# Twelve low parts at the four feed-forward entries: from VectorE subtractions to accumulating transfers

## The chip, the cores and the metric

The kernel runs on one core of one Trainium2 chip. The core has TensorE (PE, with its weight loads shown apart as PEld), VectorE (DVE), ScalarE (ACT), GpSimd (POOL) and SyncE (SP), and 16 DMA engines. The time is the device time of one execution in microseconds (us), median of several runs. All durations below come from one execution taken by the hardware profiler.

## The reference

The reference computes two blocks on x of 512 tokens by 1024 channels in float32. Each block has two mixers, and each mixer is followed by a feed-forward part, so there are four of these:

```
def swiglu(h, wg, wu, wd):
    return (jax.nn.silu(h @ wg) * (h @ wu)) @ wd
```

follows the hybrid mixer and the conformer convolution (hidden size 2816), and

```
def sq_relu_mlp(x, w_up, w_down):
    return jnp.square(jax.nn.relu(x @ w_up)) @ w_down
```

follows the differential attention and the short convolution (hidden size 4096). All operands are float32, and the result must hold float32 accuracy, which is why each weight and each activation is split into a high and a low part.

## The kernel before, in words

The activations lie transposed: channels on partitions, the 512 tokens along the free side, in eight tiles of 128 channels. Each float32 matmul is made of three matmuls in the fp32r format (`mm3`, L302 to L305): high weight by high activation (L303), high weight by low activation (L304), low weight by high activation (L305). The `wl` in a row's L305 is thus the low part of a weight, and it is the last of the three that is needed.

`w_parts` (L269 to L281) makes both parts of a weight chunk of 128x1024 floats (512 KB) that lies in SBUF as loaded (`wraw`). ACT copies it into `wh`, which rounds it (all ACT rows carry line 102, since a helper issues them). Then the low part is made in one of two ways: DVE subtracts, `wl = wraw - wh` (L279); or, where the flag `low_by_dma` is set, ACT writes the chunk scaled by -1, rounded, into `wl`, and a transfer on the POOL queue adds the chunk to it in memory (L277, `accum_op=add`). Before, the flag is set in one place only, the first projection of the conformer convolution, for 16 chunks. `wh` and `wl` have four buffers each, `wraw` three (each of two chunks, 1 MB).

A feed-forward's first matrix is worked off in groups of 512 output columns. The first group is `group_plain` (L488): eight k steps of 128 rows of the weight, two halves of the tokens (`th` 0 and 1, 256 tokens each), 12 matmuls of 128x256 per k step and half, so 96 per half. Its weights are two row blocks of 1 MB, k 0 to 3 and k 4 to 7, which are four chunks #1 to #4 of two k steps each. At given k steps it calls other work (norms: L423 in the swiglu, L1127 in the MLP, both on PE at th 0 behind k 3). All further groups are `group_s` (L513): a scheme with seven block products in place of eight, each product 24 matmuls of 128x256 with one weight chunk of 128x4x256. Its blocks b11, b12, b21, b22 are halves of two loaded `wraw` buffers, and sums of them are formed in place on DVE: b11 becomes b12-b11 (L530), b12 becomes b22-b12 (L539), b22 becomes b11-b22 with the new b11 (L540). The first product is called o11 here and uses b11 as loaded; the second uses the new b11 (b11' here), the third the new b22 (b22' here), the fourth b22 as loaded (o22 here).

I call the start of a feed-forward, `group_plain` and the first `group_s` behind it, an entry. In the profile PE begins the plain group of the four entries at about 304 us (swiglu 1), 873 us (swiglu 2), 1488 us (MLP 1) and 2040 us (MLP 2). Around an entry DVE also makes the low parts of the activations (L430, L435, L456), the sums of activations that `group_s` multiplies (L454 to L464), the squares' sum of the norm (L412), and takes the results from PSUM (L849, L852 in the swiglu). In the MLP, DVE applies the norm before it (L1135, L1136, with the factor `rm` that ACT makes from PE's L1127). A scheduler (the Tile framework) orders the instructions of each engine from the program's dependences; an engine works its own list in order, so an instruction that waits holds all behind it.

Of the kernel before, what the change touches and what calls it, by code (L numbers as in the profile page):

```python
# [109 lines left out]
def body(ctx: ExitStack, tc: tile.TileContext, A, out, consts):  # L110
# [11 lines left out]
    def bank(tag="mm"):  # L122
        n_ps[0] += 1
        return pp.tile([P, T], F32, tag=tag, name=f"ps{n_ps[0]}", bufs={"mm": 4, "at": 4}[tag])
# [11 lines left out]
    def F(n=1):  # L136
        r = [fslots.pop(0) for _ in range(n)]
        return r if n > 1 else r[0]
# [126 lines left out]
    n_p = [0]  # L265

    low_by_dma = [False]

    def w_parts(src, n):  # L269
        n_p[0] += 1  # L270
        wh = wpool.tile([P, 1024], F32R, tag="wh", name=f"wh{n_p[0]}", bufs=4)
        wl = wpool.tile([P, 1024], F32R, tag="wl", name=f"wl{n_p[0]}", bufs=4)
        v = (lambda t: t[:, :n]) if len(src.shape) == 2 else (lambda t: t[:, :n].rearrange("p (k c) -> p k c", k=src.shape[1]))
        act.activation(v(wh), src, AF.Copy)
        if low_by_dma[0]:
            act.activation(v(wl), src, AF.Copy, scale=-1.0)
            pool_e.dma_start(out=v(wl), in_=src, accum_op=ALU.add)  # L277
        else:
            dve.tensor_sub(v(wl), src, v(b(wh)))  # L279
        return wh, wl  # L280
# [21 lines left out]
    def mm3(ps, wh, wl, h, l, start, stop):  # L302
        pe.matmul(ps, wh, h, start=start, stop=False, skip_group_check=True)  # L303
        pe.matmul(ps, wh, l, start=False, stop=False, skip_group_check=True)  # L304
        pe.matmul(ps, wl, h, start=False, stop=stop, skip_group_check=True)  # L305
# [168 lines left out]
    def load_blocks(w0, w1):  # L474

        rvs = []
        for kh in range(2):
            n_w[0] += 1
            raw = wpool.tile([P, 2048], F32, tag="wraw", name=f"wraw{n_w[0]}", bufs=3)
            rv = raw[:, :].rearrange("p (k c) -> p k c", k=4)  # L480
            rows = slice(kh * 512, (kh + 1) * 512)
            if w0[0] is w1[0] and w1[1] == w0[1] + 256:
                sync.dma_start(rv, w0[0][rows, w0[1] : w0[1] + 512].rearrange("(k p) c -> p k c", p=P))
            else:
                for n, (ap, c) in enumerate((w0, w1)):
                    sync.dma_start(rv[:, :, n * 256 : (n + 1) * 256], ap[rows, c : c + 256].rearrange("(k p) c -> p k c", p=P))
            rvs.append(rv)
        return rvs  # L488

    def group_plain(w0, w1, evac, at):  # L490


        ws = []
        for rv in load_blocks(w0, w1):
            for h in range(2):
                wh, wl = w_parts(rv[:, 2 * h : 2 * h + 2, :].rearrange("p k c -> p (k c)"), 1024)
                ws += [(wh[:, k * T : (k + 1) * T], wl[:, k * T : (k + 1) * T]) for k in range(2)]
        for th, tr in enumerate((T0, T1)):
            pss = [bank(), bank()]
            for k in range(8):  # L500
                for n in range(2):
                    for p in range(2):
                        wh, wl = (t[:, n * 256 + p * P : n * 256 + (p + 1) * P] for t in ws[k])
                        mm3(pss[n][:, p * 256 : (p + 1) * 256], wh, wl, xh[k][:, tr], xl[k][:, tr], k == 0 and p == 0, k == 7)
                if (th, k) in at:
                    at[th, k]()
            for n in (1, 0):
                evac(n, th, pss[n], False)

    def group_s(w0, w1, evac):  # L510


        bb = []  # L513
        for rv in load_blocks(w0, w1):
            bb += [rv[:, :, :256], rv[:, :, 256:]]
        b11, b12, b21, b22 = bb

        def product(ps, w, x, start=False):
            for k in range(4):
                for p in range(2):  # L520
                    wh, wl = (t[:, k * 256 + p * P : k * 256 + (p + 1) * P] for t in w)
                    mm3(ps[:, p * 256 : (p + 1) * 256], wh, wl, *x(k), start and k == 0 and p == 0, k == 3)

        xs = lambda k0, tr: lambda k: (xh[k0 + k][:, tr], xl[k0 + k][:, tr])
        sums = lambda n: lambda k: (so[0][:, k, n, :], so[1][:, k, n, :])
        parts = lambda t: w_parts(t, 1024)

        a, d, g = bank(), bank("at"), bank("at")
        o11 = parts(b11)
        dve.tensor_sub(b11, b12, b11)  # L530
        product(a, o11, xs(0, T0), True)
        p1 = F()
        act.activation(p1, a, AF.Copy)

        product(g, parts(b11), sums(0), True)
        p5 = F()
        act.activation(p5, g, AF.Copy)
        o22 = parts(b22)
        dve.tensor_sub(b12, b22, b12)  # L539
        dve.tensor_sub(b22, b11, b22)  # L540
        product(a, parts(b22), sums(1))
        u2 = F()
        act.activation(u2, a, AF.Copy)
        product(g, o22, sums(2))
        dve.tensor_add(u2, g, u2)
        evac(1, 0, u2, True)
        product(a, parts(b12), xs(0, T1))
        dve.tensor_add(p5, a, p5)
        evac(1, 1, p5, True)
        product(d, parts(b21), xs(4, T0), True)  # L550
        dve.tensor_add(p1, d, p1)
        evac(0, 0, p1, True)
        dve.tensor_add(b21, b21, b22)
        product(a, parts(b21), xs(4, T1))
        evac(0, 1, a, False)
# [267 lines left out]
    def swiglu(layer, nxt):  # L823
# [15 lines left out]
        for pi, nf in enumerate(parts):  # L839
            (ph, hh), (pl, hl) = RP(nf // 2), RP(nf // 2)  # L840
            for fc in range(nf // 2):
                col = (f0 + fc * 2) * P
                ss = [None, None]

                def evac(n, th, ps, own):
                    x = HALVES[th]
                    if n == 1:
                        s = ss[th] = ps if own else F()
                        dve.tensor_mul(halves_2(s), halves_2(ps), rb[:, x].unsqueeze(1).to_broadcast([P, 2, 256]))  # L849
                        act.activation(s, s, AF.Silu)  # L850
                        return
                    dve.tensor_mul(ss[th], ps, ss[th])  # L852
                    split_to(ph[fc][:, :, x], pl[fc][:, :, x], halves_2(ss[th]))
                    freeF(ss[th])
                    if own:
                        freeF(ps)

                if pi == 0 and fc == 0:
                    group_plain((wu, col), (wg, col), evac, {(0, 3): norm, (1, 0): lambda: split_all_sums("ffnn", layer)})
                    after_first()  # L860
                else:
                    group_s((wu, col), (wg, col), evac)
# [28 lines left out]
    w1 = A["cv_w_pw1"][0]  # L891
# [496 lines left out]
    def mlp(layer, nxt, before):  # L1388
# [4 lines left out]
        for pi in range(4):  # L1393
            (ph, hh), (pl, hl) = RP(4), RP(4)
            for g in range(2):
                f0 = pi * 8 + g * 4

                def evac(n, th, ps, own):
                    s = ps if own else F()
                    act.activation(s, ps, AF.Relu)  # L1400
                    act.activation(s, s, AF.Square)
                    split_to(ph[g * 2 + n][:, :, HALVES[th]], pl[g * 2 + n][:, :, HALVES[th]], halves_2(s))
                    freeF(s)

                if pi == 0 and g == 0:
                    group_plain((wu, f0 * P), (wu, f0 * P + 256), evac, {
                        (0, 1): before.second, (1, 0): lambda: split_all_sums("fpre", layer)})
                    for k in range(4):
                        split_s3(k, V("fpre", layer * 8 + k))
                    post = Post().then("fpost", layer, nxt) if nxt else Final("fpost", layer)  # L1410
                else:
                    group_s((wu, f0 * P), (wu, f0 * P + 256), evac)
# [105 lines left out]
```

## Time and profile before

| | |
|---|---|
| median of 3 runs | 2416.68 us (2415.71 to 2418.15) |
| profiled execution | 2416.4 us, span 2414.6 us, 1.8 us around it |
| mean granted TensorE clock | 0.991 |
| PE busy | 2362.9 us, 98% |
| DVE busy | 1562.3 us, 65% |
| ACT busy | 1195.4 us, 50% |
| POOL busy | 228.0 us, 9% |

The busy share tells that PE hardly ever idles. It idles 51.7 us in all (span less busy time), most of it in 36 waits, and the table of waits says which instruction of which engine ended them. A row of a timeline has the start, the duration, the engine, the line, the operation, the tiles (output first) and, in brackets, how long the engine was idle before and what ended that.

### The profile page before, as it was taken

How to read it: one execution, taken by the hardware profiler on the slowest of the kernel's cores; microseconds unless marked ns; L12 is line 12 of the kernel's file. 1: busy time of each engine (PE TensorE's matmuls, PEld its weight loads, DVE VectorE, ACT ScalarE, POOL GpSimd, SP SyncE). 2: the span in 40 equal slices, each digit the busy share in tenths (PEclk: the TensorE clock that was granted, in tenths of full speed). 3: DMA queues.
4: the chain of work that ended last, by engine and by line, in shares of the span. 5: the costliest groups of instructions: out<-in, count | busy, mean ns of one | idle time of the engine just before them, and what ended most of it. 6: DMA issues, size and time to landing. Idle time of an engine off the chain costs nothing. (4 is left out here: it accounts for less than half of the span.)

```text
span 2414.6 us, 34306 instructions
## 1 busy us (share of the span) xinstructions
PE 2362.9 (98%) x14087; PEld 2051.1 (85%) x14087; DVE 1562.3 (65%) x2099; ACT 1195.4 (50%) x2005; POOL 228.0 (9%) x206
## 2 busy tenths in 40 slices
PE   8999999999999899999999999899998999999998
PEld 6667798999887799898987778798898888888997
DVE  4334685867699978685746775664577544854664
ACT  4663463434675654352534555653554224653553
POOL 0000000111113110202000003100003102100001
PEclk9999999999999999999999999999999999999999
DMA  5112223242563023232331112222332222222330
GB/s 167 36 53 68 73 72 121 73 135 73 135 153 97 19 87 123 70 127 84 116 105 58 48 53 71 88 88 88 122 105 70 96 96 88 73 76 96 123 105 36
DMA packets 150415, 215.30 MB, mean 89 GB/s; under 512 B 6079, under 2 KB 88562, under 8 KB 150258
## 3 DMA queue, kind: packets, MB, share of 16 engines
q1 hardware_dynamic: 147921, 204.72, 26.3%
q0 software_dynamic: 2304, 8.39, 1.8%
q8 instruction: 110, 1.80, 0.3%
q14 instruction: 48, 0.39, 0.0%
q10 hardware_dynamic: 32, 0.01, 0.0%
HBM read 202.61 MB, written 2.10 MB: 85 GB/s over the span
## 5 line engine op out<-in xcount | busy, mean ns | idle before, releaser
L303 PE MATMUL ps<-rs,wh 128*128 128x256 f32 (+1 forms) x3216 | 1083.8, 337 | 10.4 <-ACT rs L102 5.1
L305 PE MATMUL ps<-rs,wl 128*128 128x256 f32 (+1 forms) x3216 | 1080.2, 336 | 10.3 <-DVE wl L279 10.3
L304 PE MATMUL ps<-rs,wh 128*128 128x256 f32 (+1 forms) x3216 | 1081.2, 336 | 0.0
L279 DVE TENSOR_TENSOR wl<-wraw,wh 128x1024 fp32r<-128x1024 f32 (+1 forms) x472 | 576.6, 1230 | 473.9 <-ACT wh L102 472.3
L102 ACT ACTIVATE wh<-wraw 128x1024 fp32r<-128x1024 f32 (+1 forms) x488 | 508.3, 1047 | 665.6 <-PE ps L304 528.1
L303 PEld LDWEIGHTS ps<-rs,wh 128*128 128x128 f32 x3216 | 609.9, 190 | 78.1 <-ACT rs L102 5.9
L305 PEld LDWEIGHTS ps<-rs,wl 128*128 128x128 f32 x3216 | 610.6, 190 | 77.1 <-DVE wl L279 11.8
L304 PEld LDWEIGHTS ps<-rs,wh 128*128 128x128 f32 x3216 | 610.4, 190 | 67.2 <-issue 2.9
L102 ACT ACTIVATE fs<-fs 128x512 f32<-128x512 f32 (+2 forms) x365 | 205.3, 571 | 87.8 <-DVE fs L1168 20.2
L305 PE MATMUL ps<-ph_so,wl 128*128 128x256 f32 x816 | 234.7, 288 | 3.1 <-DVE wl L279 2.9
L303 PE MATMUL ps<-ph_so,wh 128*128 128x256 f32 x816 | 233.3, 286 | 4.0 <-ACT wh L102 3.5
L304 PE MATMUL ps<-ph_so,wh 128*128 128x256 f32 x816 | 232.5, 285 | 0.0
L102 ACT ACTIVATE fs<-ps 128x512 f32<-128x512 f32 (+1 forms) x202 | 112.5, 561 | 136.3 <-PE ps L305 105.6
L305 PEld LDWEIGHTS ps<-ph_so,wl 128*128 128x128 f32 x816 | 158.2, 194 | 6.6 <-DVE wl L279 6.6
L303 PEld LDWEIGHTS ps<-ph_so,wh 128*128 128x128 f32 x816 | 158.4, 194 | 5.1 <-ACT wh L102 4.2
L304 PEld LDWEIGHTS ps<-ph_so,wh 128*128 128x128 f32 x816 | 158.1, 194 | 0.0
L102 ACT ACTIVATE rs<-fs 128x512 fp32r<-128x512 f32 (+1 forms) x153 | 91.9, 606 | 77.1 <-DVE fs L852 45.3
L435 DVE TENSOR_TENSOR rs<-fs,rs 128x512 fp32r<-128x512 f32 (+1 forms) x132 | 86.5, 662 | 17.2 <-ACT rs L102 16.8
L868 POOL TENSOR_TENSOR fs<-fs,fs 128x512 f32<-128x512 f32 x32 | 52.2, 1631 | 474.2 <-DVE fs L866 474.2
L102 ACT ACTIVATE rs<-fs,vec 128x256 fp32r<-128x256 f32 (+1 forms) x104 | 58.5, 585 | 62.6 <-POOL fs L1136 19.1
L412 POOL TENSOR_TENSOR fs<-fs,fs 128x512 f32<-128x512 f32 x28 | 46.5, 1662 | 382.3 <-ACT fs L102 376.2
L1106 POOL TENSOR_TENSOR fs<-fs,fs 128x256 f32<-128x256 f32 (+1 forms) x33 | 35.4, 1072 | 363.0 <-ACT fs L102 356.6
(310 smaller groups left out, 2209.7 us busy)
## 6 DMA issues: line engine op xcount, KB each, us to landing
wraw<-in_mlp_w_up_dram SPq DMA_DIRECT2D x32, 1024.0 KB
wraw<-in_mlp_w_down_dram SPq DMA_DIRECT2D x32, 1024.0 KB
wraw<-in_ffn_w_up_dram SPq DMA_DIRECT2D x44, 512.0 KB
wraw<-in_ffn_w_gate_dram SPq DMA_DIRECT2D x44, 512.0 KB
wraw<-in_ffn_w_down_dram SPq DMA_DIRECT2D x20, 1024.0 KB
wraw<-in_cv_w_pw_dram SPq DMA_DIRECT2D x16, 512.0 KB
wl<-wraw POOLq DMA_DIRECT2D x16, 512.0 KB, 5.3
wraw<-in_attn_w_qkv_dram SPq DMA_DIRECT2D x16, 512.0 KB
```

The costliest lines, as they stand in the source:

```text
L102: r = self.engine.activation(out, in_, func, **kw)
L279: dve.tensor_sub(v(wl), src, v(b(wh)))
L303: pe.matmul(ps, wh, h, start=start, stop=False, skip_group_check=True)
L304: pe.matmul(ps, wh, l, start=False, stop=False, skip_group_check=True)
L305: pe.matmul(ps, wl, h, start=False, stop=stop, skip_group_check=True)
L412: r = eng.tensor_add(acc, acc, s)
L435: dve.tensor_sub(l, src, b(h))
L868: pool_e.tensor_add(res[o], res[o], s)
L1106: pool_e.tensor_add(self.acc[:, tr], self.acc[:, tr], s[:, tr])
```

## The change

A second flag, `after_plain`, is added. In `group_plain`, the chunks of the second row block (#3 and #4, k 4 to 7) get their low parts by the accumulating transfer, and so does o11 of the first `group_s` behind it. That is three chunks at each of four entries: 12 subtractions on DVE (L279) go, 12 ACT copies and 12 POOL transfers (L277) come. No load and no matmul is added or removed.

```diff
+    after_plain = [False]
...
-        for rv in load_blocks(w0, w1):
+        for i, rv in enumerate(load_blocks(w0, w1)):
+
+            low_by_dma[0] = i == 1
             for h in range(2):
                 wh, wl = w_parts(rv[:, 2 * h : 2 * h + 2, :].rearrange("p k c -> p (k c)"), 1024)
...
+        low_by_dma[0] = False
+        after_plain[0] = True
...
         a, d, g = bank(), bank("at"), bank("at")
+        low_by_dma[0], after_plain[0] = after_plain[0], False
         o11 = parts(b11)
+        low_by_dma[0] = False
         dve.tensor_sub(b11, b12, b11)
```

The flags add lines, so a line of the kernel before stands 1 higher in the changed one from L267 on and 7 higher from L530 on (L279 becomes L280, L530 becomes L537).

DVE at entry 1, before, from the low part of o11 (`wl_2354`, from `wraw_2344`) to L540:

```order
L279 TENSOR_TENSOR wl_2354<-wraw_2344,wh_2353 128x1024
L456 SCALAR_TENSOR_TENSOR rs_69<-fs_99,vec,rs_65 128x256
L456 SCALAR_TENSOR_TENSOR rs_70<-fs_108,vec,rs_66 128x256
L530 TENSOR_TENSOR wraw_2344<-wraw_2344 128x4x256
L456 SCALAR_TENSOR_TENSOR rs_70<-fs_109,vec,rs_66 128x256
L539 TENSOR_TENSOR wraw_2344<-wraw_2347,wraw_2344 128x4x256
L279 TENSOR_TENSOR wl_2384<-wraw_2344,wh_2383 128x1024
L279 TENSOR_TENSOR wl_2413<-wraw_2347,wh_2412 128x1024
L540 TENSOR_TENSOR wraw_2347<-wraw_2344,wraw_2347 128x4x256
```

The same place on DVE after the change (L537, L546 and L547 are L530, L539 and L540 of before; L856 and L859 are L849 and L852):

```order
L457 SCALAR_TENSOR_TENSOR rs_69<-fs_99,vec,rs_65 128x256
L457 SCALAR_TENSOR_TENSOR rs_70<-fs_108,vec,rs_66 128x256
L457 SCALAR_TENSOR_TENSOR rs_70<-fs_109,vec,rs_66 128x256
L537 TENSOR_TENSOR wraw_2346<-wraw_2346 128x4x256
L546 TENSOR_TENSOR wraw_2346<-wraw_2349,wraw_2346 128x4x256
L280 TENSOR_TENSOR wl_2387<-wraw_2346,wh_2386 128x1024
L856 TENSOR_TENSOR fs_101<-ps_2200,fs_92 128x512
L280 TENSOR_TENSOR wl_2416<-wraw_2349,wh_2415 128x1024
L859 TENSOR_TENSOR fs_101<-ps_2199,fs_101 128x512
L547 TENSOR_TENSOR wraw_2349<-wraw_2346,wraw_2349 128x4x256
```

The subtraction of o11 has gone. L537 overwrites b11, which the transfer of o11 reads, so it waits for that transfer's landing. The two evacuations L856 and L859 now stand ahead of the sum L547.

ACT at entry 3 after the change, around chunks #3 (`wl_12559`) and #4 (`wl_12564`) of the plain group:

```order
L102 ACTIVATE wh_12558<-wraw_12548 128x1024
L102 ACTIVATE fs_105<-fs_109 128x256
L102 ACTIVATE rs_68<-fs_88,vec 128x256
L102 ACTIVATE wl_12559<-wraw_12548 128x1024
L102 ACTIVATE wh_12563<-wraw_12548 128x1024
L102 ACTIVATE wl_12564<-wraw_12548 128x1024
L102 ACTIVATE fs_100<-ps_12594,epsc 128x256
```

The two `wl` copies are new; without them the list is that of before. The last row is the first step of `rm`, and both copies stand ahead of it. On POOL the three transfers of an entry stand in a row, here those of entry 1:

```order
L278 DMA wl_2067<-wraw_2055 128x1024
L278 DMA wl_2072<-wraw_2055 128x1024
L278 DMA wl_2356<-wraw_2346 128x4x256
```

All three are new. PE's list is that of before but for one matmul with the low part of chunk #3 at entries 3 and 4, which moves a few places back, so that two matmuls more stand ahead of the first use of that chunk's low part. SP's list is unchanged.

## Rows read from the trace of the kernel before

**Rows 1.** Page, part 1: busy time, share of the span, instructions of each engine.
```profile
PE 2362.9 (98%) x14087; PEld 2051.1 (85%) x14087; DVE 1562.3 (65%) x2099; ACT 1195.4 (50%) x2005; POOL 228.0 (9%) x206
```
**Rows 2.** Waits of PE, whole span: line, waited for, us in total, times, longest.
```profile
PE ps L305 <- DVE wl L279: 13.3, 11, 2.7
```
**Rows 3.** Waits of PE, 1480 to 1540 us (entry 3).
```profile
PE ps L305 <- DVE wl L279: 6.5, 4, 2.7
```
**Rows 4.** Waits of PE, 2036 to 2090 us (entry 4).
```profile
PE ps L305 <- DVE wl L279: 5.4, 4, 2.7
...
PE ps L1127 <- POOL fs L1106: 1.1, 1, 1.1
```
**Rows 5.** Waits of PE, 284 to 370 us (entry 1).
```profile
PE ps L423 <- DVE fs L412: 0.6, 1, 0.6
```
**Rows 6.** Low parts, 640 to 770 us, count, ns min/median/max; last row landing in us.
```profile
L102 ACT ACTIVATE wl<-wraw x16: 1039/1044/1053, 646.9 to 753.9; 128x1024 fp32r<-128x1024 f32 x16
L277 POOL DMA_DIRECT2D wl<-wraw x16: 850/862/1176, 648.3 to 756.5; - x16
...
DMA to landing us min/median/max: 4.4/5.3/9.7
```
**Rows 7.** Timeline of ACT at 648 us: start, us, line, operation, tiles.
```profile
648.81 1.04 ACT L102 ACTIVATE wl<-wraw 128x1024 fp32r<-128x1024 f32 x1
```
**Rows 8.** Timeline of POOL at 650 us.
```profile
650.16 0.86 POOL L277 DMA_DIRECT2D wl<-wraw  x1 [0.86 <-ACT wl L102]
```
**Rows 9.** Timeline of DVE, 316 to 332 us (entry 1).
```profile
316.97 0.69 DVE L849 TENSOR_TENSOR fs<-ps,fs 128x512 f32<-128x512 f32 x1 [0.28 <-PE ps L305]
...
322.73 1.22 DVE L530 TENSOR_TENSOR wraw<-wraw 128x1024 f32<-128x1024 f32 x1
...
330.20 1.23 DVE L279 TENSOR_TENSOR wl<-wraw,wh 128x1024 fp32r<-128x1024 f32 x1 [0.59 <-ACT wh L102]
331.35 0.68 DVE L852 TENSOR_TENSOR fs<-ps,fs 128x512 f32<-128x512 f32 x1
```
**Rows 10.** Timeline of ACT, 319 to 330 us (entry 1).
```profile
319.70 1.06 ACT L102 ACTIVATE wh<-wraw 128x1024 fp32r<-128x1024 f32 x1
...
329.11 1.06 ACT L102 ACTIVATE wh<-wraw 128x1024 fp32r<-128x1024 f32 x1 [2.65 <-DVE wraw L540]
```
**Rows 11.** Timeline of DVE at 884 us (entry 2).
```profile
884.49 0.69 DVE L849 TENSOR_TENSOR fs<-ps,fs 128x512 f32<-128x512 f32 x1 [0.62 <-PE ps L305]
```
**Rows 12.** Timeline of PE, 1512 to 1522 us (entry 3).
```profile
1512.87 0.28 PE L304 MATMUL ps<-rs,wh 128*128 128x256 f32 x1
...
1515.36 0.28 PE L304 MATMUL ps<-rs,wh 128*128 128x256 f32 x1
...
1518.71 0.42 PE L303 MATMUL ps<-rs,wh 128*128 128x256 f32 x1
...
1521.28 0.41 PE L303 MATMUL ps<-rs,wh 128*128 128x256 f32 x1
```
**Rows 13.** Stretches: us, PE, PEld, DVE, ACT, POOL busy, PEclk, DMA share, GB/s.
```profile
1498.00:1500.00 2.00, 2.00 (x19) 2.00 (x18) 2.00 (x4) 0.94 (x3) 1.18 (x2) 1.00 1.04 397
...
1520.00:1530.00 10.00, 7.36 (x40) 6.75 (x39) 9.13 (x11) 7.79 (x14) 4.11 (x2) 0.75 0.00 0
```
**Rows 14.** Timeline of ACT, 1492 to 1505 us (entry 3).
```profile
1492.16 1.04 ACT L102 ACTIVATE wh<-wraw 128x1024 fp32r<-128x1024 f32 x1
...
1504.76 1.06 ACT L102 ACTIVATE fs<-ps 128x512 f32<-128x512 f32 x2
```
**Rows 15.** Timeline of PE at 1495 us (entry 3, k 4 of th 0).
```profile
1495.54 0.29 PE L305 MATMUL ps<-rs,wl 128*128 128x256 f32 x1
```
**Rows 16.** Timeline of DVE, 1496 to 1518 us (entry 3).
```profile
1496.46 0.88 DVE L1135 SCALAR_TENSOR_TENSOR fs<-fs,vec,fs 128x256 f32<-128x256 f32 x2 [0.48 <-ACT fs L102]
...
1504.50 0.48 DVE L1135 SCALAR_TENSOR_TENSOR fs<-fs,vec,fs 128x256 f32<-128x256 f32 x1
...
1517.07 1.22 DVE L279 TENSOR_TENSOR wl<-wraw,wh 128x1024 fp32r<-128x1024 f32 x1
```

## Prediction

> **What bounds the kernel now.** I read the busy shares first: PE works in 98% of the span, every other engine has room [rows 1]. So the time is PE's own work plus its gaps, and an edit away from PE counts only where it opens or closes a gap. The change takes low parts from DVE, so the table of waits is next: PE waits for a low part by DVE (L279) 13.3 us in 11 places [rows 2]. Cut to the four entries, the table gives 6.5 us of these to entry 3 [rows 3] and 5.4 to entry 4, which also has 1.1 at L1127 [rows 4]. Entry 1 has 0.6 at L423, for the sums L412 on DVE, and no wait for a low part [rows 5]; entry 2 has no wait at all. So there is something to win at entries 3 and 4, 0.6 at entry 1, and at entry 2 only something to lose.
>
> Then the price of the new way, which the conformer convolution shows 16 times: an ACT copy of 1.04 us, an issue of 0.86 on POOL, and a landing 4.4 to 9.7 us after the issue began, median 5.3 [rows 6]. POOL's issue at 650.16 follows the ACT copy that began at 648.81 and ended at 649.85, so 0.3 lies between [rows 7, 8]. From the start of the copy to the landing it is 1.0 + 0.3 + 4.4 to 5.3, some 6.2 us, where DVE took 1.23 [rows 9]. I take 4.9 for a landing, between minimum and median, as three transfers an entry do not crowd the queue. The 16 were 128x1024 in one piece; o11 is four pieces a partition (128x4x256), which the trace does not show, so its landing may lie anywhere from 4.4 to 9.7, and below 4.4 if fewer bytes in flight help it.
>
> **Entries 1 and 2 (swiglu).** Chunks #3 and #4: DVE loses two passes and so reaches L412 about 0.8 us earlier, which closes the 0.6 at L423. Their landings come at about 309.7 and 312.5 us by the same steps, about when k 4 and k 6 begin; I count nothing for them.
>
> o11, entry 1. PE ends th 0 at about 316.9, when it releases L849 [rows 9]; less the 0.6, 316.4. Half th 1 is 96 matmuls at 0.119 (21 steps from 1512.87 to 1515.36 [rows 12]), 11.4 us, so PE wants o11 at 327.8. ACT's copy into wh began at 319.70 [rows 10]: 0.6 earlier now, plus 1.0, one small copy of 0.4 and the new copy of 1.0 end at 321.6; the issue is at 321.9, the landing at 326.8. PE does not wait for it.
>
> But DVE does. L530 overwrites b11, which the transfer reads. It began at 322.73 [rows 9] and now begins at 326.9. Behind it on DVE's list stand L539, the low part of b11', L849, the low part of o22, L852 and L540, then ACT's copy of b22' and its low part. From rows, 1.14 to 1.2 for each of the five 128x1024 passes before ACT (331.35 less 330.20 [rows 9] is the spacing) and 0.6 for each evacuation: 326.9 + 5.8 + 1.2 puts L540's end at 333.9. ACT's copy takes 1.06 behind it (it waited for L540 in the kernel before too [rows 10]), DVE's pass 1.23: b22' is ready at 336.4. PE wants it after two products of 24 matmuls (2.86 each) and two more matmuls, 327.8 + 5.95 = 333.8. Before, it was ready at 331.4 [rows 9]. A gap of 2.6 us opens; less the 0.6, entry 1 loses 2.0.
>
> Entry 2 runs the same list 567.5 us later [rows 9, 11], without a wait to close: th 0 ends at 884.45, o11 is due at 895.9, landing 894.9, gap 2.6. It loses 2.6.
>
> Clock: behind the 2.7 us gap of entry 3, twelve matmuls from 1518.71 to 1521.28 stand 0.214 apart [rows 12], which is the granted clock's lower level, 1.2 GHz in place of 2.4; the stretch behind has a mean of 0.75 [rows 13]. Such a piece costs 1.5 us (twelve times 0.214, and so many fewer at 0.119: 12 x 0.095 = 1.1, with the neighbours at the edges some 1.5). Of the two new gaps I count it for one: 1.5.
>
> **Entries 3 and 4 (MLP).** What the two plain passes free on DVE buys nothing there. L1135 at 1496.46 waited for ACT's rm, which comes from PE's L1127 [rows 16], so DVE resumes at the same time. Chunk #3: ACT begins its wl copy at 1492.16, in the place of wh of #4 [rows 14]; issue 1493.4, landing 1497.8 to 1498.7, later if the 1 MB load that fills the DMA engines at 1498 (share 1.04 [rows 13]) is in the way. PE wants it at 1495.54 [rows 15] plus the two matmuls that move ahead, 1495.8. PE waits 2.0 to 2.9, say 2.5. #4 lands at about 1500.2, wanted at 1501.2.
>
> So th 0 ends 2.5 later, and ACT's evacuation at 1504.76 [rows 14], which stood 0.9 behind PE (o11's 1515.2 less 11.4 is 1503.8), moves 1.6. From 1504.50 DVE works without a gap up to o11's low part at 1517.07 [rows 16], 30 instructions; in the new list 18 of them stand ahead of the last sum that ACT's copy follows, 18 x 0.419 = 7.5, so 1512.0. Splits on ACT 1.3, the wl copy 1.0, 0.3, landing 4.9: 1519.5, or 1521.1 if the 1.6 goes through, against 1518.3 before. PE wants o11 at 1517.9 by then. The loss is 1.2 to 2.8, I take 2.0. If landings are 0.5 shorter and the queue of sums is shorter, it is 0.6; with a second stretch at 1.2 GHz 4.
>
> Entry 4 is the same code. Its 1.1 at L1127 may go, as POOL's sum has DVE's passes no longer beside it, but rm's first step stands behind both copies on ACT, and #3's landing is late as at entry 3. Also 2.0.
>
> **Sum.** 2.0 + 2.6 + 1.5 + 2.0 + 2.0 = 10.1 on the profiled execution's 2416.4 (2414.6 span and 1.8 around it): 2426.5. The median of the runs is 0.3 higher, so 2426.8, slower by 0.4%. The 12 DVE passes that go, 14.8 us of DVE's time, are not in the sum: DVE is no bound where it waits for a landing.
>
> The page "DMA: Bandwidth & Descriptors" of the Trainium skill, section "Anatomy of one DMA — SWDGE (gpsimd) path", fits such a transfer at 2.0 us plus its bytes at 436 GB/s: an estimate of 3.2 us for 512 KB. The trace disagrees for its 16, none of which landed under 4.4 [rows 6]; by the page each landing would be 1.7 earlier, and the sum 6.8 less, with the stretch at 1.2 GHz gone too about 2.
>
> **Rivals.** A: the relief on DVE is carried through. For it: DVE is busy in every stretch of entries 3 and 4, and o11's low part is the longest wait of each, 2.7 [rows 3, 4]. If o11 lands before PE wants it at both, 2 x 2.7 goes, with the two stretches at 1.2 GHz behind them (1.5 each) and the 0.6 and 1.1: about 9 less, 2407. It decides from a landing before 1515.4, that is an ACT copy done by 1510. Against it: ACT's copy stands behind sums that DVE ends at 1512.
>
> B: landings are late. For it: 9.7 was seen when loads ran [rows 6], the loads run at entries 3 and 4 [rows 13], and o11 comes in smaller pieces. With 7.1 for o11 (midway of 4.4 and 9.7) each entry loses 2.2 more, 8.8, and with a stretch at 1.2 GHz at all four, 4.5 more, 2440; with the clock alone 2431, which I count to the forecast.
>
> C: the landings are shorter than any of the 16, as a transfer of which three are alone on the queue may be; the issue alone is 0.86 [rows 6], and nearest to that 3.0 is still thinkable. The four chains end 1.9 earlier each, 7.6, no new stretch at 1.2 GHz, 1.5: the sum is 1.0, 2417 to 2418. That also holds where slack hides two of the four. The page's fit above would come out here.
>
> **Numbers.** Forecast 0.54, B 0.17, C 0.20, A 0.09. About 0.2% (4.8 us) is what a measurement of this kernel can tell from no change: A is faster, C within it, forecast and B slower: 0.09, 0.20, 0.71. The forecast's own range is 2421 to 2432 (landings 4.4 or 5.9, no or three stretches at 1.2 GHz). The range that leaves out A and the far half of B is 2415 to 2437.
>
> **What would show it.** In the changed profile: at entries 1 and 2 a DVE wait of about 4 us at L537 that ends with a landing, a new PE wait at L306 or L304 of b22' of some 2.6 us, and none at o11; the 0.6 at L423 gone. At entry 3 a PE wait of 2 to 3 us at k 4 for the transfer, and the wait at o11 released by the transfer in place of DVE, near 1520. PE waits for L280 fall, waits for transfers take their place. Wrong would be: L537 without a wait (the landing before DVE comes, C or A), no new gap at b22', or a PE start of o11 at entry 3 under 1517 (A).

## The result and the profile after

The changed kernel takes 2433.43 us (median of 4 runs, 2430.04 to 2437.68) against 2416.19 us for the kernel before (median of 4 runs, 2413.66 to 2418.15). The ratio is 1.0072, 95% interval 1.0057 to 1.0087: slower by 17 us. The forecast was 2426.8 with a range of 2415 to 2437: the right side, inside the range, 6.6 us too small and 1.4 above the forecast's own range of 2421 to 2432.

The page of the changed kernel, part 1, against [rows 1]:

```profile
PE 2369.6 (97%) x14087; PEld 2053.7 (84%) x14087; DVE 1550.0 (64%) x2087; ACT 1205.4 (50%) x2017; POOL 237.3 (10%) x218
```

DVE has twelve instructions less and works 12.3 us less, ACT has twelve more and works 10.0 us more (twelve passes of 1.23 and 1.04 us would be 14.8 and 12.5). PE's busy time grows by 6.7 us though it runs the same matmuls, so they ran at the lower clock for longer (mean granted clock 0.989 against 0.991). The rest of the span's 15.9 us (2430.5 less 2414.6), 9.2 us, are new gaps. The waits of PE over the whole span (us in total, times, longest), against [rows 2]:

```profile
PE ps L306 <- DMA wl<-wraw: 12.4, 4, 3.5
PE ps L306 <- DVE wl L280: 9.6, 11, 1.8
PE ps L304 <- ACT wh L102: 8.2, 6, 1.7
```

Waits for DVE's low parts fell from 13.3 to 9.6, and four waits for transfers, 12.4 us, came in their place. Cut to the entries, they stand in two groups. At entry 1 (DVE, then PE; a bracket gives the idle time before and what ended it):

```profile
319.96 0.48 DVE L457 SCALAR_TENSOR_TENSOR rs<-fs,vec,rs 128x256 fp32r<-128x256 f32 x1 [0.18 <-ACT rs L102]
324.24 1.22 DVE L537 TENSOR_TENSOR wraw<-wraw 128x1024 f32<-128x1024 f32 x1 [3.80 <-DMA wl<-wraw]
```
```profile
332.47 0.39 PE L304 MATMUL ps<-ph_so,wh 128*128 128x256 f32 x1 [1.66 <-ACT wh L102]
333.73 0.39 PE L306 MATMUL ps<-ph_so,wl 128*128 128x256 f32 x1 [0.76 <-DVE wl L280]
```

DVE stands still for 3.80 us until the transfer of o11 has read b11, and PE then has a gap of 2.42 us ahead of the third product. There was none before: the one wait of entry 1 was the norm's [rows 5]. Entry 2 has the same pair at 904.35 and 905.61, with 1.66 and 0.76. The transfers of entry 1, on POOL:

```profile
302.22 1.06 POOL L278 DMA_DIRECT2D wl<-wraw  x1 [5.26 <-ACT wl L102]
305.08 0.86 POOL L278 DMA_DIRECT2D wl<-wraw  x1 [1.80 <-ACT wl L102]
319.15 1.30 POOL L278 DMA_DIRECT2D wl<-wraw  x1 [13.22 <-ACT wl L102]
```

The last is o11: issued at 319.15, landed when L537 begins, 5.1 us later. At entries 3 and 4 PE waits twice for a transfer at each, for chunk #3 and for o11:

```profile
1505.19 0.58 PE L306 MATMUL ps<-rs,wl 128*128 128x256 f32 x1 [2.36 <-DMA wl<-wraw]
...
1526.71 0.39 PE L306 MATMUL ps<-rs,wl 128*128 128x256 f32 x1 [3.07 <-DMA wl<-wraw]
```
```profile
2061.09 0.55 PE L306 MATMUL ps<-rs,wl 128*128 128x256 f32 x1 [3.49 <-DMA wl<-wraw]
...
2083.24 0.58 PE L306 MATMUL ps<-rs,wl 128*128 128x256 f32 x1 [3.51 <-DMA wl<-wraw]
```

The landings (min/median/max of the three) are 4.4/4.6/5.1 at entry 1 and, at entries 3 and 4:

```profile
DMA to landing us min/median/max: 5.1/7.5/8.1
```
```profile
DMA to landing us min/median/max: 5.5/8.8/9.4
```

To see what each entry costs, I took its length in each profile, from a row at its start (the first L812 on DVE, the first L1079 on DVE, the first wait of the plain group on PE for the MLP) to the third in-place sum L530 behind it. In the kernel before these are 79.28, 82.39, 118.13 and 117.55 us. The table has the difference to that, and the waits of PE in the two MLP entries in brackets (9.19 and 9.38 before). What is left of a span's difference lies mostly at the program's start: up to the first row of entry 1, where the code is the same in all, the nine profiles take 280.5 to 286.2 us, at mean granted clocks of 0.99 to 0.97. So the entries are compared here, and not the spans. Each ratio is to runs of the kernel before made beside that kernel's (medians 2416.2 us for the changed kernel, 2415.9 for the next four, 2417.2 for the last three).

| kernel | median us, ratio (95%) | entry 1 | entry 2 | entry 3 | entry 4 |
|---|---|---|---|---|---|
| changed | 2433.4, 1.0072 (1.0057 to 1.0087) | +4.24 | +3.00 | +2.98 (11.19) | +8.91 (13.11) |
| o11 alone | 2427.2, 1.0044 (1.0031 to 1.0056) | +5.97 | +4.28 | +0.70 (8.13) | -0.61 (8.11) |
| #3 and #4 alone | 2424.0, 1.0033 (1.0021 to 1.0045) | -0.05 | -0.06 | +4.68 (10.94) | +4.73 (12.49) |
| o11 from HBM | 2431.8, 1.0064 (1.0052 to 1.0076) | +0.05 | +0.34 | +4.73 (11.48) | +9.22 (15.47) |
| load held back | 2432.4, 1.0067 (1.0054 to 1.0079) | +4.34 | +4.47 | +3.24 (9.83) | +2.02 (11.70) |
| #4 alone | 2420.5, 1.0016 (1.0007 to 1.0024) | -0.81 | +0.04 | +2.54 (9.46) | +1.94 (8.87) |
| o11 alone, MLP only | 2417.1, 0.9997 (0.9988 to 1.0006) | +0.23 | +0.01 | +1.09 (8.14) | -0.70 (7.86) |
| the same, o11 early | 2413.1, 0.9981 (0.9973 to 0.9990) | 0.00 | +0.04 | -2.28 (7.67) | -1.63 (7.70) |

### The profile page after: what moved, and what is told of

It is laid out like the page before. It is cut to its first block, busy times and chain, and to the rows that moved or that the text cites. A ratio compares the mean times of both kernels' runs of the same rounds, so it can differ in the third digit from the quotient of the medians.

```text
span 2430.5 us, 34334 instructions
## 1 busy us (share of the span) xinstructions
PE 2369.6 (97%) x14087; PEld 2053.7 (84%) x14087; DVE 1550.0 (64%) x2087; ACT 1205.4 (50%) x2017; POOL 237.3 (10%) x218
## 5 line engine op out<-in xcount | busy, mean ns | idle before, releaser
L306 PE MATMUL ps<-rs,wl 128*128 128x256 f32 (+1 forms) x3216 | 1080.5, 336 | 17.3 <-DMA wl<-wraw 12.4
L280 DVE TENSOR_TENSOR wl<-wraw,wh 128x1024 fp32r<-128x1024 f32 (+1 forms) x460 | 562.2, 1231 | 471.6 <-ACT wh L102 470.3
L413 POOL TENSOR_TENSOR fs<-fs,fs 128x512 f32<-128x512 f32 x28 | 45.8, 1636 | 358.4 <-ACT fs L102 352.4
L431 DVE SCALAR_TENSOR_TENSOR rs<-fs,vec,rs 128x256 fp32r<-128x256 f32 (+1 forms) x88 | 62.9, 735 | 11.5 <-ACT rs L102 11.5
```

Of the source, the lines that this page charges most:

```text
L413: r = eng.tensor_add(acc, acc, s)
L431: dve.scalar_tensor_tensor(xl[k][:, x], res[k][:, x], gain, b(xh[k][:, x]), ALU.mult, ALU.subtract)
```

## The experiments

### o11 alone

```diff
-            low_by_dma[0] = i == 1
+            low_by_dma[0] = False
```

Expected: 

> Undoes the plain group's part: chunks 3 and 4 of the plain groups get their low parts on VectorE as before, only the first block product's weights (o11) go by the accumulating transfer, at all four entries. Theory 1 (at the swiglu entries the loss comes from VectorE's in-place sum, which must wait until o11's transfer has read its block): the two swiglu entries lose the same as in the changed kernel, a gap of 2.4 us ahead of the third product at each, some 3 to 4 us each with a stretch at the lower clock. Theory 2 (at the MLP entries the loss comes from chunks 3 and 4, whose transfers land late beside a 1 MB load): without them the MLP entries lose at most 3 us each, since o11 alone lands some 3 us after VectorE's pass ended before; the sum is +9 to +13, 2425 to 2429 us. Rival (o11 carries the MLP entries' loss as well): the MLP entries keep 3.0 and 8.9, the sum stays at +16 to +18, 2432 to 2434.

Measured: 2427.2 us, in the expected range. The gap at the swiglu entries is that of the changed kernel, 1.67 and 0.76 us ahead of the third product at both. At entry 1:

```profile
337.27 0.39 PE L304 MATMUL ps<-ph_so,wh 128*128 128x256 f32 x1 [1.67 <-ACT wh L102]
338.53 0.58 PE L306 MATMUL ps<-ph_so,wl 128*128 128x256 f32 x1 [0.76 <-DVE wl L280]
```

These two entries cost 6.0 and 4.3 us, more than the 3 to 4 expected. The MLP entries cost next to nothing, and PE waits 1.1 and 1.3 us less there than before, the wait for o11 being 2.47 and 2.45 in place of 2.7 and some small ones behind it gone. So the loss at the swiglu entries is o11's, and at the MLP entries it is not. The rival fell.

### Chunks #3 and #4 alone

```diff
-        low_by_dma[0], after_plain[0] = after_plain[0], False
+        after_plain[0] = False
```

Expected: 

> Undoes o11's part: o11's low part is VectorE's subtraction as before, only chunks 3 and 4 of the plain groups go by transfers, at all four entries. Theory 1: no gap ahead of the third product at the swiglu entries, which then gain 0.3 (less wait for the norm) and 0. Theory 2: the waits of 2.4 and 3.5 us for chunk 3 at the MLP entries stay; TensorE's evacuation on ScalarE and with it VectorE's list move by 1.5 to 2.5, so the MLP entries lose 1.5 to 3 each; the sum is +3 to +6, 2419 to 2422 us. Rival (chunks 3 and 4 cost nothing in the end, since the wait for o11 behind them shrinks by as much): within 1 us of before, 2415 to 2417.

Measured: 2424.0 us, 2 us above the expected range; the swiglu entries are free, as expected, but the MLP entries lose 4.7 each and not 1.5 to 3. PE's waits for #3 are 2.46 and 3.60:

```profile
1500.87 0.38 PE L306 MATMUL ps<-rs,wl 128*128 128x256 f32 x1 [2.46 <-DMA wl<-wraw]
...
1521.86 0.46 PE L306 MATMUL ps<-rs,wl 128*128 128x256 f32 x1 [2.37 <-DVE wl L280]
```

The wait for o11 behind it is still 2.37, almost the 2.7 of before. The second wait does not shrink by the first, since DVE's pass for o11 comes later too. Counted from the entry's first row, PE resumes at o11 33.9 us in (30.0 before), and ACT's evacuation of PE's results begins at 19.3 (16.4 before). That the late evacuation holds DVE's list is read from the order of the lists and was not tested. Of 4.7 us, 1.8 and 3.1 are PE's waits. At entry 3 most of the rest goes with the lower clock (mean granted clock over the entry 0.93, 0.96 before); at entry 4 it is 0.96 in both, and 1.6 us stay unexplained.

### o11 from HBM

```diff
-            pool_e.dma_start(out=v(wl), in_=src, accum_op=ALU.add)
+            pool_e.dma_start(out=v(wl), in_=src if low_from is None else low_from, accum_op=ALU.add)
...
-        o11 = parts(b11)
+        o11 = w_parts(b11, 1024, w0[0][0:512, w0[1] : w0[1] + 256].rearrange("(k p) c -> p k c", p=P))
```

Expected: 

> The changed kernel, but o11's accumulating transfer adds the weight block from HBM in place of the copy in SBUF that VectorE overwrites, so the in-place sum has nothing to wait for. Theory 1: at the swiglu entries VectorE starts the sum when its other work is done (about 4 us earlier), the gap of 2.4 us ahead of the third product is gone and TensorE waits for nothing there if the landing is under 6 us; the swiglu entries cost under 0.5 us each, the MLP entries what they cost in the changed kernel: 2433 less 6 to 7, 2426 to 2427 us. Rival (the gap comes from VectorE's or ScalarE's other work, or o11's own landing becomes the wait): a gap of 2 us or more stays at the swiglu entries, 2431 to 2434.

Measured: 2431.8 us, above the expected 2426 to 2427. The swiglu entries did what the theory said: +0.05 and +0.34, and no wait is left at these two entries but the norm's 0.28 and, at the start of entry 2, one of 0.20 that the kernel before has as well. DVE at entry 1:

```profile
322.01 1.22 DVE L537 TENSOR_TENSOR wraw<-wraw 128x1024 f32<-128x1024 f32 x1 [0.46 <-ACT wl L102]
```

It waits for ACT's copy, not for a landing. So the cause at the swiglu entries is shown: the transfer reads the block that DVE overwrites in place. The median fell by 1.6 us only. At the MLP entries landings from HBM took 6.0 and 6.3 us against 5.1 and 5.5, PE's waits for o11 rose to 4.03 and 4.26 (3.07 and 3.51 in the changed kernel), and one wait for #3 was 5.12:

```profile
1523.11 0.58 PE L306 MATMUL ps<-rs,wl 128*128 128x256 f32 x1 [4.03 <-DMA wl<-in_mlp_w_up_dram]
...
2060.49 0.58 PE L306 MATMUL ps<-rs,wl 128*128 128x256 f32 x1 [5.12 <-DMA wl<-wraw]
```

These two entries lost 2.1 us more, so the four are 4.8 us shorter than in the changed kernel's profile. The span is only 0.8 shorter, and most of what is between lies ahead of entry 1, which the edit does not touch: 283.6 us here, 280.5 there. How much of the 4.8 the median holds stays open.

### The load beside the transfers held back

```diff
+            if kh == 1 and hold[0] is not None:
+                sync.dma_start(raw[:, 0:1], b(hold[0])[:, 0:1])
+                hold[0] = None
...
+        hold[0] = ws[7][1] if w0[0] is w1[0] else None
```

Expected: 

> The changed kernel, but at the two MLP entries the 1 MB load of the second block of the following group is held back until the transfer of chunk 4 has landed (a transfer of 512 bytes from that chunk's low part into the load's buffer stands ahead of it; the load overwrites it). Theory 2 (the transfers of chunks 3 and 4 land late there because that load shares the DMA engines): their landings fall from 7.5 to 9.4 us to under 6, TensorE's waits for chunk 3 (2.4 and 3.5 us) fall under 0.5, and the MLP entries lose 3 to 6 us less in sum: 2427 to 2430 us. Rival (the two transfers slow each other, or GpSimd's issue beside VectorE is slow): landings stay over 7 us, the waits stay, 2432 to 2435.

Measured: 2432.4 us, above the expected 2427 to 2430. The landings at the two MLP entries fell as the theory said:

```profile
DMA to landing us min/median/max: 4.5/5.1/5.2
```
```profile
DMA to landing us min/median/max: 5.4/5.7/6.0
```

The wait for #3 is gone at entry 3 and 1.46 us at entry 4 (3.49 in the changed kernel):

```profile
2063.24 0.39 PE L306 MATMUL ps<-rs,wl 128*128 128x256 f32 x1 [1.46 <-DMA wl<-wraw]
```

That the load makes the landings late is shown. In the changed kernel the DMA queues between 1498 and 1507 us read (packets, MB, share of the 16 engines):

```profile
q0 software_dynamic: 276, 1.04, 58.4%
q1 hardware_dynamic: 528, 1.05, 40.9%
```

The accumulating transfers and the load share the engines, which are full for the whole stretch. But the wait for o11 was 3.74 and 3.71 (3.07 and 3.51 in the changed kernel), more than with o11 alone. In both, o11's copy begins when ACT's list comes to it. Counted from the entry's first row, its issue is at 25.96 us here, 24.51 with o11 alone and 29.07 in the changed kernel, where DVE's own pass had ended at 29.96 in the kernel before. With #3's and #4's passes gone from DVE, the list of ACT puts six splits of sums ahead of the copy; with o11 alone there are four. The medians of this kernel and the changed one differ by 1 us only, within their intervals, so of the 6.6 us by which the MLP entries are shorter in this profile, at most the waits' 2.8 can be read as the load's, and what the late landings cost in the median is not shown.

### Chunk #4 alone

```diff
-            low_by_dma[0] = i == 1
             for h in range(2):
+                low_by_dma[0] = i == 1 and h == 1
```

(o11 by VectorE, as in the run of #3 and #4 alone.) Expected: 

> Only the last chunk (number 4) of each plain group gets its low part by the accumulating transfer; chunk 3 and o11 are VectorE's as before. It tells a late landing from any other cost of the transfers, since chunk 4 is wanted 24 matmuls (2.9 us) later than chunk 3 and its copy on ScalarE comes 1 us earlier without chunk 3's. Theory (chunk 3's landing, 5.4 to 8.8 us after an issue that is itself too late, makes the loss at the MLP entries): chunk 4 lands in time or under 1 us late, TensorE's wait for it is under 1 us in place of 2.4 to 3.6, and the MLP entries lose under 1.5 us each in place of 4.7: 2415 to 2419 us. Rival (any transfer beside the load of 1 MB costs the MLP entries several us, by the copies on ScalarE or the load's delay): 2421 us or more.

Measured: 2420.5 us, between the theory's 2415 to 2419 and the rival's 2421. PE does not wait for #4 at entry 3 and waits 0.42 at entry 4, though it landed after 6.1 and 7.4 us, and the waits of the MLP entries are those of before (9.46 and 8.87). So a landing that is late but not wanted yet costs no wait. The entries are 2.5 and 1.9 us longer all the same. A wait at the third product is new (1.88 and 1.96), with others shorter in its place. What differs is the mean granted clock of the two entries, 0.93 and 0.94 where it was 0.96. Whether the transfer brings this about, as the rival has it, is not settled.

### o11 of the MLP entries alone, and earlier

```diff
+        low_by_dma[0] = by_dma
+        o11 = w_parts(bb[0], 1024)
+        low_by_dma[0] = False
...
-        o11 = parts(b11)
```

(in a function of its own, called with the flag for the first group behind a plain group of the MLP). Expected: 

> Only o11 of the two MLP entries goes by the accumulating transfer; the swiglu entries and all plain groups are as before. In the run with o11 alone at all four entries TensorE's waits at the MLP entries were 8.1 us each against 9.2 and 9.4 before. Theory: the same here, a gain of 1 to 1.3 us of waits at each MLP entry, swiglu entries unchanged, 2413 to 2416 us, within 0.2% of before. Rival (the transfer at the MLP entries costs as it did with chunks 3 and 4): the MLP entries lose 3 us or more each, 2421 us or more.

Measured: 2417.1 us, ratio 0.9997 (0.9988 to 1.0006), above the expected 2413 to 2416. The waits are 8.14 and 7.86, less by 1.1 and 1.5, but no gain can be measured; the interval, -2.9 to +1.5 us, does not exclude one of that size either. The rival fell. For the last run this function is called inside the plain group, at k 2 of the second half, and the sums behind it:

```diff
-                        (0, 1): before.second, (1, 0): lambda: split_all_sums("fpre", layer)})
+                        (0, 1): before.second, (1, 3): lambda: split_all_sums("fpre", layer), (1, 2): early})
```

Expected: 

> As the run with o11 of the MLP entries alone, but o11's two copies are written into the program inside the plain group's second half, ahead of the sums of activations, so that ScalarE makes them some 1 to 2 us earlier and the landing comes at about the time when TensorE wants o11. Theory (o11's wait is then gone, but VectorE's list of sums still sets the next block sum, so the wait moves to the second product): the wait for o11 falls from 2.7 to under 0.7 us, the waits at the second product (1.6 and 0.8 before) grow to 3 or more, and the entries gain 1 to 2 us each: 2411 to 2415 us. Rival (o11's wait was the bound of these entries): the whole 2.7 us and the stretch at the lower clock behind it go at each, 2406 to 2410 us.

Measured: 2413.1 us, ratio 0.9981 (0.9973 to 0.9990), faster than both kernels, and as the theory said. PE at entry 3:

```profile
1518.90 0.39 PE L305 MATMUL ps<-rs,wl 128*128 128x256 f32 x1 [0.37 <-DMA wl<-wraw]
1524.53 0.58 PE L303 MATMUL ps<-ph_so,wh 128*128 128x256 f32 x1 [2.75 <-ACT wh L102]
1526.31 0.58 PE L305 MATMUL ps<-ph_so,wl 128*128 128x256 f32 x1 [0.99 <-DVE wl L279]
```

The wait for o11 falls from 2.70 to 0.37 (to nothing at entry 4), and the wait at the second product rises from 1.63 and 0.75 to 2.75 and 0.99. The list of sums on DVE sets the time there, and the low part of o11 is only one pass of it: at entry 3 DVE works without a gap from 1501.8 to the end of the in-place sum (from 1522.16, 1.22 us) that the second product's weights need. The edit moves the sums in the program as well as o11, so what each of the two moves is worth is not told apart.

## Why the prediction was right, and where it was too small

**The side and the two mechanisms were right.** At the swiglu entries the in-place sum waits for o11's landing (3.80 us, some 4 forecast), PE is not held at o11, and the gap opens two products later: 2.42 measured, 2.6 forecast. The landing was 5.1 where I took 4.9. The page "DMA: Bandwidth & Descriptors" of the Trainium skill gives an estimate of 3.2 by its fit (section "Anatomy of one DMA — SWDGE (gpsimd) path"). No landing of the changed kernel was under 4.4, so the traces disagree with it here. Rival C, which needed landings near 3.0, fell.

**The 0.6 at L423** fell to 0.28 only. The squares on ACT now stand behind the two new copies, so DVE waits 0.71 for them at L413.

**The clock** was right in kind and small in size. I counted one stretch of 1.5 us for two gaps. In the changed kernel's profile it was one for two, and the entries cost 7.2 us in place of 6.1. Over three profiles (the changed kernel, o11 alone, the load held back), such a gap of 2.3 to 2.4 us at a swiglu entry is followed by a stretch at the lower level at five entries of six. The mean granted clock (column 7, behind the five engines' busy times) behind the gaps of entries 1 and 2 of the changed kernel:

```profile
332.00:342.00 10.00, 8.77 (x58) 8.57 (x59) 6.72 (x6) 5.40 (x7) 0.00 (x0) 0.83 0.34 107
904.00:914.00 10.00, 8.89 (x72) 8.69 (x73) 8.23 (x8) 5.40 (x7) 0.00 (x0) 1.00 0.45 130
```

The six entries cost 3.0 to 6.0 us, 4.4 in the mean, so two together cost some 8.8 and not 6.1.

**The step that was mis-sized is the one of entries 3 and 4, "2.0 + 2.0".** It measured 3.0 + 8.9 in the profile. Three things in it failed.

First, the wait for #3 was forecast at 2.5 and came at 2.36 and 3.49, but by two errors that cancel, which is luck. I placed k 4 right behind L1127. In the MLP that norm stands behind k 1 (my description of the kernel, which says k 3, is right for the swiglu alone), so what [rows 15] shows is k 2, and #3 is wanted 2.7 us later than I said (the last matmul before the wait begins at 1502.56, with the entry 4.16 us later than before). The landing took 7.5 and 8.8 us and not 4.9, because of the load. I had [rows 13] in hand, which shows the DMA engines full there, and kept the value for a transfer that runs alone. Rival B named the load, but put its late landing (7.1) on o11, which landed after 5.1 and 5.5.

Second, I let o11 land 1.2 to 2.8 later than DVE's pass had ended, and it was 4.2. Counted from the entry's first row, PE resumes at o11 34.22 us in, and 30.01 before. The evacuation on ACT moved by 2.4 with PE's gap, not 1.6, and six splits of sums stand ahead of the copy on its list. That these two make the 4.2 is read from the lists; no run changed them alone.

Third, the clock. The forecast put no stretch at these entries. Entry 4 in the kernel before and in the changed one, over 65 us each:

```profile
2039.00:2104.00 65.00, 55.63 (x394) 52.53 (x393) 59.69 (x88) 46.98 (x82) 14.42 (x10) 0.92 0.27 87
```
```profile
2046.00:2111.00 65.00, 51.71 (x346) 49.62 (x345) 51.66 (x81) 44.45 (x78) 15.95 (x13) 0.84 0.34 88
```

The mean granted clock falls from 0.92 to 0.84, which is 5.2 us of full speed (0.08 x 65), beside 3.7 us of waits: together the 8.9. It does not add up so at every entry: with o11 alone, entry 3 has 0.93 against 0.96 before and 1.1 us less of waits, and is 0.7 longer only. The kernel before had such stretches at this entry too, and how many follow a given set of gaps changes from one execution to the next. The four timed runs of the changed kernel lie 7.6 us apart, and their mean granted clock falls from 0.990 in the fastest to 0.987 in the slowest; 0.003 of the span is 7.3 us. So one profile can't settle how the 11.9 us of the two entries divide in the median. With #3 and #4 alone, the two cost 4.7 each.

**Rival A** was rightly small: relief on DVE carried through only where o11's transfer started earlier, and then for 1.6 to 2.3 us an entry, since the next sum on DVE's list takes the wait's place.

**Two sums.** The terms of rival A add up to 10.1 (2 x 2.7, 2 x 1.5, 0.6 and 1.1), not to about 9. The forecast's own range was added up short at its upper end: four landings 1.0 later and two more stretches of 1.5 give 2433.8, not 2432, and the measured 2433.4 lies just under that.

## What to carry to other kernels

A transfer that takes over a pass from an engine also takes a reader's hold on its source for as long as it is under way. Before moving a pass, look for who writes that source next, and count what is queued behind that writer. Price a transfer by the rows of transfers that ran beside the same load as it will, not by the quiet ones, and look up in the instruction order where its result is first wanted instead of inferring it from a neighbour.

## What the runs showed of the hardware

An accumulating transfer from SBUF of 128x4x256 took POOL 1.30 us to issue where 128x1024 took 0.85 to 1.06 at the entries of the changed kernel, and landed after 5.0 to 5.5 us there; from HBM it landed after 6.0 to 6.3. Two of 512 KB beside a load of 1 MB landed after 7.5 to 9.7 us in the three kernels that have them so, and after 4.5 to 6.0 with the load held back. PE gaps of the same 2.3 to 2.4 us were followed by a stretch at 1.2 GHz at five of six entries.
